# Two more groups of weight sums made ahead, and a new order of units in four feed-forward blocks

## The chip, the cores and the metric

The kernel runs on one core of one Trainium2 chip. Its time is the device time in microseconds of one execution, and the metric is the median of several. The engines of the core are named as in the profile: PE is TensorE's matmul, PEld its weight load, DVE is VectorE, ACT is ScalarE, POOL is GpSimd, and SP is SyncE, which issues most transfers. The core has 16 DMA engines.

## The reference

One decoder layer on 256 tokens of width 2048, in float32: a first half feed-forward (f1), a pair of gated token mixers (retention and sliding-window attention), a second half feed-forward (f2), and a gated per-layer embedding, each closed by a layer norm.

```python
def swiglu(x, w_gu, w_down):
    g, u = jnp.split(x @ w_gu, 2, axis=-1)
    return (jax.nn.silu(g) * u) @ w_down

for i in range(DEPTH):                                   # DEPTH = 1
    h = layer_norm(alpha * h + 0.5 * swiglu(h, w_ffn1_gu[i], w_ffn1_down[i]), ...)
    rq, rk, rv, rg, aq, ak, av, gate_r, gate_a = jnp.split(h @ w_in[i], SPLIT_POINTS, axis=-1)
    ...                                                  # retention, attention
    mixed = (sigmoid(gate_r) * ret_branch + sigmoid(gate_a) * att_branch) @ w_mix_out[i]
    h = layer_norm(alpha * h + mixed, ...)
    h = layer_norm(alpha * h + 0.5 * swiglu(h, w_ffn2_gu[i], w_ffn2_down[i]), ...)
    h = layer_norm(alpha * h + sigmoid(h @ w_ple_gate[i]) * (p[i] @ w_ple_proj[i]), ...)
```

The change concerns the weights of the two feed-forwards: `w_gu` is 2048 x 11264 (gate and up), `w_down` 5632 x 2048.

## The kernel before, in words

**A product of float32.** Every factor is split into a high and a low part, and a product is three matmuls into one sum: low of the tokens times high of the weight (line 426), high times high (L427), high times low (L428). A matmul is 128x128 by 128x512.

**Chunks.** Weights come as raw chunks of 128x1024 float32, 512 KB each, by a transfer that SP issues (L121). ScalarE casts the raw chunk to its high part (L132), VectorE subtracts to get the low part (L136).

**Blocks and units.** A feed-forward has 11 blocks of gate and up (`f1g`, `f1u`, `f2g`, `f2u`; j = 0 to 10), each with eight pairs p of chunks, one of the gate and one of the up side, and then the down product in two blocks of 22 pairs. How a pair is worked off is a letter in a string, in the order of use:

- P, a plain pair: two chunks, cast and subtracted as above, 24 matmuls.
- T, the same, but the low part of the second chunk is made without VectorE: ScalarE copies the raw chunk with its sign turned (L141), and the subtraction is a transfer with accumulation that GpSimd issues (L142). It is begun up to three units ahead.
- S, a seven: the four quarters of the pair are combined to seven products in place of eight (as Strassen does), 21 matmuls. The sums of weights are made on VectorE (four of 128x512, L216 to L218 and L221), cast on ScalarE (`huf`, L219, and `hvf`, L222; and `bf`, L207) and subtracted on VectorE (`luf` and `lvf`, L224, L225, beside L136 and L223).
- D, a prepared seven: the same 21 matmuls, but the four parts `hu`, `lu`, `hv`, `lv` were made earlier and lie in DRAM. It loads one whole chunk (L121), half of the other (L244) and four sums of 512 KB (L248); VectorE makes two low parts only.

**Sums made ahead.** `AHEAD` lists the pairs of f2's blocks that are D. `sums_ahead` makes their four parts while the token mixers run, between f1 and f2, a step at a time: each call of `run_side`, once a unit, takes one step, and `every` is the number of units between two steps. There are five stretches of the mixers in which it is started, each with a slice of the list.

**What sets the order.** The program is written out by Python in one pass. `plan` is the list of units to come; `fill` loads, then makes them ahead of their use, as long as the slots of 128x1024 that the stretch has (`slots_for_weights`) hold them and the queued matmuls stay below `ahead` = 45 and `far` = 90 in units of `time` (12 a chunk, 21 a seven). Each engine runs its own instructions in the order written, and a load waits on SP until its slot is free. So the strings decide in which order every engine meets the work, and which load stands behind which.

**After a block** VectorE and ScalarE fold the sevens' sums (`eve`, `evw`, L535 to L541), apply the gate, and turn the result by a DMA transpose that SP issues (L982).

Of the kernel before, what the change touches and what calls it, by code (L numbers as in the profile page):

```python
# [40 lines left out]

SEVEN = (0, 1, 2, 3)

AHEAD = {1: (4, 5), 2: (4,), 3: (4, 5), 4: (4,), 5: (4, 5), 7: (4, 5)}
AHEAD_SLOTS = 32

LATE = {"f1": 9, "f2": 6}

SEVEN_DOWN = (6, 7, 8, 9)
DOWN = {  # L50
    "f1": ("TTPTTPPSTSTSPSTSPSPSPP", "PTSTSTSPSPSPSPSPSPPPPP"),
    "f2": ("TTPTTPSTSTSPSTSPSPSPSP", "PTSTSTSPSPSPSPSPSPPPPP"),
}
FORMS_AT = (2, 6, 10, 14)
# [10 lines left out]
def layer(ctx: ExitStack, tc: tile.TileContext, io):  # L65
# [16 lines left out]
    def slot(shape, dt, name):  # L82
        return slots.tile(shape, dt, tag="slot", name=name)
# [179 lines left out]
    def sums_ahead(items, wait, every):  # L263


        def pause():
            for _ in range(every):
                yield

        pairs = [[Chunk(k) for k in items[0]]]  # L270
        for _ in range(wait):
            yield
        for j, (key, _) in enumerate(items):
            a, b = pairs.pop()
            b11, b21, b12, b22 = a.of(a.raw, 0), a.of(a.raw, 1), b.of(b.raw, 0), b.of(b.raw, 1)
            u, v = (slot([P, 2, 512], F32, w + a.name) for w in "uv")
            t1, t3, t2, t4 = (x.rearrange("p (g n) -> p g n", g=2) for x in (u[:, 0], u[:, 1], v[:, 0], v[:, 1]))
            parts = [slot([P, 2, 512], F32R, w + a.name) for w in ("hu", "lu", "hv", "lv")]
            uh, ul, vh, vl = parts
            away = [dram.tile([P, 2, 512], F32, name=f"{w}{a.name}") for w in ("hud", "lud", "hvd", "lvd")]  # L280
            put_by_sums[key] = away
            dve.tensor_tensor(t1, b11, b12, ALU.add)
            dve.tensor_tensor(t3, b12, b22, ALU.add)
            yield from pause()
            act.copy(uh, u)
            dve.tensor_tensor(t2, b11, t3, ALU.add)
            dve.tensor_tensor(t4, t2, b21, ALU.add)
            yield from pause()
            act.copy(vh, v)
            if j + 1 < len(items):  # L290
                pairs.append([Chunk(k) for k in items[j + 1]])
            dve.tensor_tensor(ul, u, uh, ALU.subtract)
            yield from pause()
            dve.tensor_tensor(vl, v, vh, ALU.subtract)
            for e in range(2):
                sync.dma_start(away[e], parts[e].bitcast(F32))
            yield from pause()
            for e in range(2, 4):
                sync.dma_start(away[e], parts[e].bitcast(F32))
# [52 lines left out]
    def slots_for_weights(n, ahead=45, far=90):  # L352
        room.update(slots=n, ahead=ahead, far=far)
# [5 lines left out]
    lazy = []  # L359
# [158 lines left out]
    def forms_of(parts, name):  # L518
        hi, lo = (slot([P, 8, P], F32R, name + w) for w in "hl")
        return seven_forms(whole(parts, name + "w"), hi, lo)  # L520

    def units_of(order, sevens, ahead=()):

        sevens, ahead = list(sevens), list(ahead)
        plain = [p for p in range(KD // 2) if p not in sevens + ahead]
        of = {"S": sevens, "D": ahead, "P": plain, "T": plain}
        return [(kind, of[kind].pop(0)) for kind in order]
# [399 lines left out]
    def gu_units(name, j):  # L927
        if j == 0:
            return [("P", p) for p in range(KD // 2)]
        if name == "f2" and j in AHEAD:  # L930
            if j > 4:
                return units_of("PSDSSDSP", SEVEN, AHEAD[j])
            return units_of(*(("PPSDSDSP", SEVEN[:3]) if j % 2 else ("PPSSDSSP", SEVEN)), AHEAD[j])
        return units_of("PTSSTSST" if j >= LATE[name] else "PTSSPSST", SEVEN)

    def gu_keys(name, j):
        return lambda n, p: (name + "_gu", j, n, p)
# [17 lines left out]
    def plan_ffn(name):  # L955
        for j in range(KF // 4):
            block_units(gu_units(name, j), gu_keys(name, j))
        first, second, held = down_units(name)
        block_units(first, down_keys(name, 0))
        block_units(second, down_keys(name, 1))  # L960
        plan.extend(Single(down_keys(name, 1)(n, p)) for n in range(2) for p in held)
# [30 lines left out]
    def ffn(name, i, ht, norm, keep, residual, keepers, away):  # L992
# [31 lines left out]
        for j in range(KF // 4):  # L1024
            extra = seven_banks(f"{name}{j}") if j and j % 2 == 0 else None
            pg, pu = banks(f"{name}g{j}"), banks(f"{name}u{j}")
            units = gu_units(name, j)
            n_of = {(0, 0): KD, (0, 1): KD, (1, 0): KD, (1, 1): KD}
            for kind, p in units:
# [15 lines left out]
            def before(u, j=j, offset=KD // 2 - len(units)):  # L1045
# [7 lines left out]
                if j == 0 and u == 7:  # L1053
# [3 lines left out]
                    if name == "f2":  # L1057
                        g = AHEAD[1][0] // 2
                        made[g] = forms_of([ht[:, 4 * g : 4 * g + 4, :]], f"{name}f{g}")
                if name == "f2" and j in AHEAD and u == 0:  # L1060
                    slots_for_weights(AHEAD_SLOTS - j)
# [151 lines left out]
    def mixers(ht, norm, residual, keepers, away):  # L1213
# [23 lines left out]
        def values(blk, ps):  # L1237
            hi, lo = (slot([P, 2, 512], F32R, f"rv{w}{blk}") for w in "hl")
            if isinstance(ps, list):
                for t in range(2):  # L1240
                    split(hi[:, t], lo[:, t], ps[t])
            else:
                split(hi, lo, ps)
            rv[blk] = hi, lo
# [16 lines left out]
        for n in range(2):  # L1261
            values(3 * n, ps[n])
        ahead = [(gu_keys("f2", j)(0, p), gu_keys("f2", j)(1, p)) for j in AHEAD for p in AHEAD[j]]
        slots_for_weights(22)
# [2 lines left out]
        made.clear()  # L1267
        slots_for_weights(14)
        lazy.append(rotary_table("a"))
        lazy.append(sums_ahead(ahead[0:2], 2, 2))  # L1270
        for j in range(4):
            bank(f"pass{j}")
        rq[:] = [slot([P, 4, S], F32, f"rq{j}") for j in range(2)]
# [108 lines left out]
        def two_heads(h, at=0):  # L1382
            steps = (
                ret1(h), both(ret1b(h), ret1(h + 1)), both(ret1b(h + 1), ret2(h)),
                both(ret2b(h), ret2(h + 1)), ret2b(h + 1),
            )
            for j, step in enumerate(steps):
                along(at + j, step)

        two_heads(0)  # L1390
        lazy.append(sums_ahead(ahead[2:5], 2, 3))
        for h in range(0, HR, 2):
            ps = banks(f"rg{h}")
            paired_out(("w_in_f2", grp), KD, rhs, ps)
# [132 lines left out]
            attention_features(grp)  # L1527

        slots_for_weights(14)
        lazy.append(sums_ahead(ahead[5:7], 0, 2))  # L1530
        sig = []
        for j in range(4):
            if j == 3:
# [46 lines left out]
            split(mt[:, :, :S], mt[:, :, S:], x)  # L1580

        slots_for_weights(14)
        lazy.append(sums_ahead(ahead[7:8], 0, 2))
        for j in range(4):
            v = sig[4 + j]
            act.activation(v, v, AF.Sigmoid)
# [7 lines left out]
        for b in range(2):  # L1594
# [3 lines left out]
            for n in range(2):  # L1598
                j = 2 * b + n
# [13 lines left out]

        lhs = lambda k: of_pairs(mix_t, k)
        slots_for_weights(16)
        lazy.append(sums_ahead(ahead[8:], 3, 2))
        for blk in range(3):
            if blk == 2:
                load_for_norm(1)
# [328 lines left out]
```

## Time and profile before

| what | value |
|---|---|
| median of 3 runs | 2231.51 us (2230.23 to 2231.71) |
| profiled execution | 2232.14 us, span 2230.3 us |
| granted clock of TensorE | 0.999 |
| PE busy | 2221.0 us, 10150 instructions |
| DVE busy | 1993.9 us, 89% of the span |
| ACT busy | 1434.9 us, 64% |
| transfers by hardware queue q1, most issued by SP | 530.68 MB, 71.5% of 16 engines |
| transfers with accumulation by GpSimd (q0) | 28.32 MB, 6.8%, 54 issues |
| block 9 of f2 | 1817.50 to 1858.30 us |
| first down block of f1 | its last seven near 559 us |

The profile is of one execution. An instruction's row gives its start, its duration, the engine, the line, and result and factors by the program's names, without buffer numbers. A bracket at the end of a row is idle time before it and what ended it. A row of a window gives its length, the busy time of PE, PEld, DVE, ACT and POOL with their counts, the granted clock, the share of the 16 DMA engines that is busy, and GB/s. In the trace matmuls overlap: the duration of one is longer than the distance between two.

### The profile page before, as it was taken

How to read it: one execution, taken by the hardware profiler on the slowest of the kernel's cores; microseconds unless marked ns; L12 is line 12 of the kernel's file. 1: busy time of each engine (PE TensorE's matmuls, PEld its weight loads, DVE VectorE, ACT ScalarE, POOL GpSimd, SP SyncE). 2: the span in 40 equal slices, each digit the busy share in tenths (PEclk: the TensorE clock that was granted, in tenths of full speed). 3: DMA queues.
4: the chain of work that ended last, by engine and by line, in shares of the span. 5: the costliest groups of instructions: out<-in, count | busy, mean ns of one | idle time of the engine just before them, and what ended most of it. 6: DMA issues, size and time to landing. Idle time of an engine off the chain costs nothing.

```text
span 2230.3 us, 28863 instructions
## 1 busy us (share of the span) xinstructions
PE 2221.0 (100%) x10150; PEld 1838.2 (82%) x10150; DVE 1993.9 (89%) x2649; ACT 1434.9 (64%) x1691; POOL 49.2 (2%) x63
## 2 busy tenths in 40 slices
PE   9999999999999999999999999999999999999998
PEld 8888888888888888888788888888888888888887
DVE  7999999989898998898979888699999999899878
ACT  6776777786655644566866556466658677866553
POOL 0000000000000000000000000000000000000000
PEclk9999999999999999999999999999999999999999
DMA  9788787997777668986957669798989989967771
GB/s 314 228 257 250 224 259 233 250 269 232 246 286 243 228 212 294 275 270 204 274 165 243 238 202 334 271 302 259 314 258 275 315 243 259 266 226 250 286 283 67
DMA packets 295929, 563.41 MB, mean 253 GB/s; under 512 B 94300, under 2 KB 98780, under 8 KB 295784
## 3 DMA queue, kind: packets, MB, share of 16 engines
q1 hardware_dynamic: 286024, 530.68, 71.5%
q0 software_dynamic: 7776, 28.32, 6.8%
q10 hardware_dynamic: 1984, 2.58, 0.4%
q8 instruction: 79, 1.29, 0.2%
q14 instruction: 66, 0.54, 0.1%
HBM read 484.43 MB, written 29.36 MB: 230 GB/s over the span
## 4 chain that ended last, share of the span: by engine, by line
PE 92%; DVE 4%; ACT 2%; issue 1%; DMA 1%; SPq 0%; ACTq 0%; DVEq 0%
PE f1g L428 3%; PE f1g L426 3%; PE f1g L427 3%; PE rqk L377 3%; PE f2g L426 2%; PE f2g L427 2%; PE f2g L428 2%; PE f1u L428 2%; PE f1u L426 2%; PE f1u L427 2%; PE f2u L427 2%; PE f2u L426 2%; PE f2u L428 2%; PE aqk L377 2%; PE gt L426 1%; PE f2d L428 1%
## 5 line engine op out<-in xcount | busy, mean ns | idle before, releaser
L132 ACT CAST hf_gu<-rf_gu 128x1024 fp32r<-128x1024 f32 x262 | 268.9, 1046 | 28.8 <-DMA rf_gu<-in_f_gu 28.1
L136 DVE TENSOR_TENSOR lf_gu<-rf_gu,hf_gu 128x1024 fp32r<-128x1024 f32 x228 | 272.7, 1219 | 11.6 <-ACT hf_gu L132 10.8
L132 ACT CAST hf_down<-rf_down 128x1024 fp32r<-128x1024 f32 x145 | 148.3, 1047 | 54.5 <-DMA rf_down<-in_f_down 45.2
L136 DVE TENSOR_TENSOR lw_in_f<-rw_in_f,hw_in_f 128x1024 fp32r<-128x1024 f32 x140 | 166.9, 1218 | 3.5 <-ACT hw_in_f L132 3.3
L136 DVE TENSOR_TENSOR lf_down<-rf_down,hf_down 128x1024 fp32r<-128x1024 f32 x125 | 149.9, 1220 | 7.7 <-ACT hf_down L132 6.7
L132 ACT CAST hw_in_f<-rw_in_f 128x1024 fp32r<-128x1024 f32 x140 | 142.0, 1050 | 18.0 <-DMA rw_in_f<-in_w_in_f 15.0
L222 ACT CAST hvf_gu<-vf_gu 128x1024 fp32r<-128x1024 f32 x78 | 82.3, 1055 | 82.6 <-DVE vf_gu L221 70.1
L219 ACT CAST huf_gu<-uf_gu 128x1024 fp32r<-128x1024 f32 x78 | 82.0, 1051 | 54.8 <-DVE uf_gu L217 51.3
L224 DVE TENSOR_TENSOR luf_gu<-uf_gu,huf_gu 128x1024 fp32r<-128x1024 f32 x78 | 95.1, 1219 | 4.7 <-ACT huf_gu L219 4.7
L225 DVE TENSOR_TENSOR lvf_gu<-vf_gu,hvf_gu 128x1024 fp32r<-128x1024 f32 x78 | 95.1, 1219 | 0.0
L428 PE MATMUL f1g<-lf_gu,xt 128*128 128x512 f32 x232 | 90.5, 390 | 0.3 <-DVE lf_gu L136 0.3
L426 PE MATMUL f1g<-hf_gu,xt 128*128 128x512 f32 x232 | 90.4, 390 | 0.0
L427 PE MATMUL f1g<-hf_gu,xt 128*128 128x512 f32 x232 | 90.3, 389 | 0.0
L426 PE MATMUL f2g<-hf_gu,ht 128*128 128x512 f32 x208 | 81.1, 390 | 0.0
L428 PE MATMUL f2g<-lf_gu,ht 128*128 128x512 f32 x208 | 81.0, 389 | 0.0
L427 PE MATMUL f2g<-hf_gu,ht 128*128 128x512 f32 x208 | 80.9, 389 | 0.0
L426 PE MATMUL f1u<-hf_gu,xt 128*128 128x512 f32 x192 | 74.7, 389 | 0.0
L427 PE MATMUL f1u<-hf_gu,xt 128*128 128x512 f32 x192 | 74.7, 389 | 0.0
L428 PE MATMUL f1u<-lf_gu,xt 128*128 128x512 f32 x192 | 74.7, 389 | 0.0
L142 POOL DMA_DIRECT2D lf_gu<-rf_gu x34 | 29.5, 867 | 1707.4 <-DMA rf_gu<-in_f_gu 1097.0
L377 PE MATMUL rqk<-ht,hw_in_f 128*128 128x512 f32 x256 | 64.3, 392 | 0.0
L426 PE MATMUL f2u<-hf_gu,ht 128*128 128x512 f32 x160 | 62.5, 391 | 0.0
(1632 smaller groups left out, 6870.5 us busy)
## 6 DMA issues: line engine op xcount, KB each, us to landing
rf_gu<-in_f_gu SPq DMA_DIRECT2D x360, 512.0 KB
rf_down<-in_f_down SPq DMA_DIRECT2D x176, 512.0 KB
rw_in_f<-in_w_in_f SPq DMA_DIRECT2D x148, 512.0 KB
lf_gu<-rf_gu POOLq DMA_DIRECT2D x34, 512.0 KB, 7.9
rw_rv<-in_w_rv SPq DMA_DIRECT2D x32, 512.0 KB
rw_ret<-in_w_ret SPq DMA_DIRECT2D x32, 512.0 KB
rw_mix<-in_w_mix SPq DMA_DIRECT2D x32, 512.0 KB
rw_pg<-in_w_pg SPq DMA_DIRECT2D x32, 512.0 KB
```

The lines of the kernel that those rows point to most:

```text
L132: act.copy(self.hi, self.raw)
L136: dve.tensor_tensor(self.lo, self.raw, self.hi, ALU.subtract)
L142: pool.dma_start(self.lo, self.raw.bitcast(F32R), accum_op=ALU.add)
L219: act.copy(uh, u)
L222: act.copy(vh, v)
L224: dve.tensor_tensor(ul, u, uh, ALU.subtract)
L225: dve.tensor_tensor(vl, v, vh, ALU.subtract)
L377: pe.matmul(ps[f], hi[:, kk, f * P : (f + 1) * P], rhs(k), start=k == 0, stop=k == n_k - 1,)
L426: pe.matmul(o, al, bh, start=first, stop=False)
L427: pe.matmul(o, ah, bh, start=False, stop=False)
L428: pe.matmul(o, ah, bl, start=False, stop=self.left == 0)
```

## The change

- `AHEAD` gains pairs 4 and 5 of block 9: twelve groups in place of ten. The slices of the five stretches become 3, 3, 2, 2 and 2 groups in place of 2, 3, 2, 1 and 2; in the fourth stretch a step is taken every unit in place of every second.
- f2's block 9 goes from "PTSSTSST" to "TDSSDSST": the pairs 4 and 5 are prepared sevens, pairs 6 and 7 have a low part by transfer, and three such pairs become two. The first seven is the third unit in both.
- f2's blocks 5 and 7 go from "PSDSSDSP" to "PDSSDSSP".
- f1's first down block goes to eight sevens from seven, and gets the string that f2's has.

```diff
--- before.py
+++ after.py
@@ -41,14 +41,14 @@
 
 SEVEN = (0, 1, 2, 3)
 
-AHEAD = {1: (4, 5), 2: (4,), 3: (4, 5), 4: (4,), 5: (4, 5), 7: (4, 5)}
+AHEAD = {1: (4, 5), 2: (4,), 3: (4, 5), 4: (4,), 5: (4, 5), 7: (4, 5), 9: (4, 5)}
 AHEAD_SLOTS = 32
 
 LATE = {"f1": 9, "f2": 6}
 
 SEVEN_DOWN = (6, 7, 8, 9)
 DOWN = {
-    "f1": ("TTPTTPPSTSTSPSTSPSPSPP", "PTSTSTSPSPSPSPSPSPPPPP"),
+    "f1": ("TTPTTPSTSTSPSTSPSPSPSP", "PTSTSTSPSPSPSPSPSPPPPP"),
     "f2": ("TTPTTPSTSTSPSTSPSPSPSP", "PTSTSTSPSPSPSPSPSPPPPP"),
 }
 FORMS_AT = (2, 6, 10, 14)
@@ -928,8 +928,10 @@
         if j == 0:
             return [("P", p) for p in range(KD // 2)]
         if name == "f2" and j in AHEAD:
+            if j == 9:
+                return units_of("TDSSDSST", SEVEN, AHEAD[j])
             if j > 4:
-                return units_of("PSDSSDSP", SEVEN, AHEAD[j])
+                return units_of("PDSSDSSP", SEVEN, AHEAD[j])
             return units_of(*(("PPSDSDSP", SEVEN[:3]) if j % 2 else ("PPSSDSSP", SEVEN)), AHEAD[j])
         return units_of("PTSSTSST" if j >= LATE[name] else "PTSSPSST", SEVEN)
 
@@ -1267,7 +1269,7 @@
         made.clear()
         slots_for_weights(14)
         lazy.append(rotary_table("a"))
-        lazy.append(sums_ahead(ahead[0:2], 2, 2))
+        lazy.append(sums_ahead(ahead[0:3], 2, 2))
         for j in range(4):
             bank(f"pass{j}")
         rq[:] = [slot([P, 4, S], F32, f"rq{j}") for j in range(2)]
@@ -1388,7 +1390,7 @@
                 along(at + j, step)
 
         two_heads(0)
-        lazy.append(sums_ahead(ahead[2:5], 2, 3))
+        lazy.append(sums_ahead(ahead[3:6], 2, 3))
         for h in range(0, HR, 2):
             ps = banks(f"rg{h}")
             paired_out(("w_in_f2", grp), KD, rhs, ps)
@@ -1527,7 +1529,7 @@
             attention_features(grp)
 
         slots_for_weights(14)
-        lazy.append(sums_ahead(ahead[5:7], 0, 2))
+        lazy.append(sums_ahead(ahead[6:8], 0, 2))
         sig = []
         for j in range(4):
             if j == 3:
@@ -1580,7 +1582,7 @@
             split(mt[:, :, :S], mt[:, :, S:], x)
 
         slots_for_weights(14)
-        lazy.append(sums_ahead(ahead[7:8], 0, 2))
+        lazy.append(sums_ahead(ahead[8:10], 0, 1))
         for j in range(4):
             v = sig[4 + j]
             act.activation(v, v, AF.Sigmoid)
@@ -1613,7 +1615,7 @@
 
         lhs = lambda k: of_pairs(mix_t, k)
         slots_for_weights(16)
-        lazy.append(sums_ahead(ahead[8:], 3, 2))
+        lazy.append(sums_ahead(ahead[10:], 3, 2))
         for blk in range(3):
             if blk == 2:
                 load_for_norm(1)
```

TensorE has 9946 rows in place of 9955. Two places show how the order of the other engines moves. The names end in block, side (0 gate, 1 up) and pair, and a buffer number.

SP, the loads of block 9 around the transpose of block 7's result (`f27t`), before:

```order
L121 DMA rf2_gu_9_0_4_16258<-in_f2_gu 128x2x512
L121 DMA rf2_gu_9_1_4_16274<-in_f2_gu 128x2x512
L982 DMA_TRANSPOSE f27t_16276<-f27w_16145 128x16x128
L121 DMA rf2_gu_9_0_5_16303<-in_f2_gu 128x2x512
L121 DMA rf2_gu_9_1_5_16305<-in_f2_gu 128x2x512
L121 DMA rf2_gu_9_0_0_16339<-in_f2_gu 128x2x512
L121 DMA rf2_gu_9_1_0_16341<-in_f2_gu 128x2x512
```

The same place of the changed kernel:

```order
L121 DMA rf2_gu_9_0_6_16320<-in_f2_gu 128x2x512
L121 DMA rf2_gu_9_1_6_16336<-in_f2_gu 128x2x512
L984 DMA_TRANSPOSE f27t_16338<-f27w_16207 128x16x128
L121 DMA rf2_gu_9_0_4_16368<-in_f2_gu 128x2x512
L244 DMA rf2_gu_9_0_4b_16370<-in_f2_gu 128x2x256
L248 DMA huf2_gu_9_0_4_16372<-hudf2_gu_9_0_4_12484 128x1024
L248 DMA luf2_gu_9_0_4_16374<-ludf2_gu_9_0_4_12485 128x1024
L248 DMA hvf2_gu_9_0_4_16376<-hvdf2_gu_9_0_4_12486 128x1024
L248 DMA lvf2_gu_9_0_4_16378<-lvdf2_gu_9_0_4_12487 128x1024
L121 DMA rf2_gu_9_0_0_16409<-in_f2_gu 128x2x512
L121 DMA rf2_gu_9_1_0_16411<-in_f2_gu 128x2x512
```

Between the transpose and the first seven's chunks (pair 0) stand six loads in place of two.

ScalarE, the end of block 9, with the third and the fourth seven (pairs 2 and 3) and the last pair (7), before:

```order
L219 CAST huf2_gu_9_0_2_16567<-uf2_gu_9_0_2_16565 128x1024
L222 CAST hvf2_gu_9_0_2_16569<-vf2_gu_9_0_2_16566 128x1024
L132 CAST hf2_gu_9_0_7_16596<-rf2_gu_9_0_7_16538 128x1024
L141 ACTIVATE lf2_gu_9_1_7_16598<-rf2_gu_9_1_7_16582 128x1024
L219 CAST huf2_gu_9_0_3_16603<-uf2_gu_9_0_3_16601 128x1024
L222 CAST hvf2_gu_9_0_3_16605<-vf2_gu_9_0_3_16602 128x1024
```

The same place of the changed kernel:

```order
L132 CAST hf2_gu_9_0_3_16648<-rf2_gu_9_0_3_16644 128x1024
L207 CAST bf2_gu_9_0_3_16650<-rf2_gu_9_1_3_16646 128x512
L219 CAST huf2_gu_9_0_3_16654<-uf2_gu_9_0_3_16652 128x1024
L222 CAST hvf2_gu_9_0_3_16656<-vf2_gu_9_0_3_16653 128x1024
L132 CAST hf2_gu_9_0_7_16692<-rf2_gu_9_0_7_16690 128x1024
L141 ACTIVATE lf2_gu_9_1_7_16723<-rf2_gu_9_1_7_16696 128x1024
L132 CAST hf2_gu_10_0_4_16726<-rf2_gu_10_0_4_16698 128x1024
```

The last pair's first cast and its sign-turning copy (L141) stood ahead of the fourth seven's casts `huf` and `hvf`, and now stand behind them.

## The prediction, made before the changed kernel had run

> **What bounds the kernel now.** I read the page first, then the waits of TensorE, then windows of 20 to 41 us cut at block borders, then single rows at the places the change touches.
>
> ```profile
> span 2230.3 us, 28863 instructions
> PE 2221.0 (100%) x10150; PEld 1838.2 (82%) x10150; DVE 1993.9 (89%) x2649; ACT 1434.9 (64%) x1691; POOL 49.2 (2%) x63
> PE 92%; DVE 4%; ACT 2%; issue 1%; DMA 1%; SPq 0%; ACTq 0%; DVEq 0%
> ...
> PE rv L426 <- DVE ht L792: 0.8, 1, 0.8
> PE f1d0s L428 <- DVE lvf_down L225: 0.2, 1, 0.2
> ```
>
> TensorE is busy for 2221.0 of 2230.3 us and holds 92% of the chain; behind the start no wait exceeds 0.8 us. A gain has to come out of the number of matmuls. A loss can come from any other engine or queue that starts to hold TensorE back, because nothing is idle behind it.
>
> **The price of a matmul** is the distance between two starts, not the printed duration.
>
> ```profile
> 1844.73 0.39 PE L428 MATMUL f2u<-bf_gu,f2fh 128*128 128x512 f32 x1
> 1844.95 0.39 PE L426 MATMUL f29s<-huf_gu,f2fl 128*128 128x512 f32 x1
> ...
> 1846.32 0.39 PE L426 MATMUL f29s<-hvf_gu,f2fl 128*128 128x512 f32 x1
> ```
>
> Seven steps lie between the first and the last of these rows: 1.59 / 7 = 0.227 us each. The change removes nine matmuls of this kind: a plain pair is 24, a seven or a prepared seven 21, so two pairs of block 9 and one of f1's first down block give three each. **Term 1: 9 x 0.227 = -2.0 us.**
>
> **f1's first down block** gets the string that f2's has already. Today its seventh seven is late:
>
> ```profile
> 558.00 0.39 PE L427 MATMUL f1d0s<-huf_down,f1forms 128*128 128x512 f32 x1
> ...
> 559.41 0.51 PE L428 MATMUL f1d0s<-lvf_down,f1forms 128*128 128x512 f32 x1 [0.17 <-DVE lvf_down L225]
> 559.75 0.40 PE L426 MATMUL f1d0s<-huf_down,f1forms 128*128 128x512 f32 x1
> ...
> L428 PE MATMUL f2d0s<-lvf_down,f2forms x8: 389/389/389, 1935.4 to 2004.7; 128*128 128x512 f32 x8
> ```
>
> Five steps took 1.75 us where 5 x 0.227 = 1.13 was due: 0.6 us lost. In f2, eight sevens in the new order show 389 ns for every one of the matmuls that wait longest for VectorE. **Term 2: -0.6 us** (0 if f1's VectorE is late all the same).
>
> **The sums made ahead** go from ten groups to twelve, one of them more in the first stretch of the mixers and one in the fourth, the `ma` blocks from 1225 us, where the pause between its steps falls from two to one. A group's own VectorE work is four sums of 128x512 and two differences of 128x1024; their prices come from the spacing of starts:
>
> ```profile
> 1825.48 1.22 DVE L225 TENSOR_TENSOR lvf_gu<-vf_gu,hvf_gu 128x1024 fp32r<-128x1024 f32 x1
> 1826.62 1.22 DVE L1072 TENSOR_TENSOR evw<-eve,evw 128x1024 f32<-128x1024 f32 x1
> 1827.75 0.69 DVE L216 TENSOR_TENSOR uf_gu<-rf_gu 128x512 f32<-128x512 f32 x1
> 1828.35 0.69 DVE L217 TENSOR_TENSOR uf_gu<-rf_gu,rf_gu 128x512 f32<-128x512 f32 x1
> ...
> 963.09 0.56 DVE L108 TENSOR_TENSOR rsp<-rsc,rsp 128x384 fp32r<-128x384 f32 x1
> 964.39 0.40 PE L1316 MATMUL ro<-rvh,rsp 128*128 128x256 f32 x2
> ...
> 1240.00:1300.00 60.00, 60.00 (x267) 49.67 (x266) 45.88 (x53) 33.11 (x36) 0.00 (x0) 1.00 0.68 232
> ```
>
> 1.135 us for the wide, 0.60 for the narrow: 4 x 0.60 + 2 x 1.135 = 4.7 us a group. The second new group has 14 us of VectorE to itself in the last row, a window (VectorE busy 45.88 of 60). For the first the thinnest cover I found is the score tile `rsp`, done at 963.65 and read at 964.39, 0.74 us ahead. If one operation of 1.135 slips ahead of it, 0.4 us show. **Term 3: +0.4 us** (0 to 4.7, a whole group).
>
> **Block 9, VectorE.** Up to the fourth seven VectorE has as much to do as before: a plain pair (2 x 1.135) and two pairs with a transfer (1.135 each) made 4.5 us, now one such pair and two prepared sevens (1.135 + 0.60 each) make 4.6. TensorE gets there earlier by six matmuls, 1.36 us, and the lead is this:
>
> ```profile
> 1847.01 1.22 DVE L225 TENSOR_TENSOR lvf_gu<-vf_gu,hvf_gu 128x1024 fp32r<-128x1024 f32 x1
> 1849.49 0.39 PE L428 MATMUL f29s<-lvf_gu,f2fh 128*128 128x512 f32 x1
> ```
>
> 1849.49 - 1848.23 = 1.26 us, so 0.1 to 0.2 are short. f1's rows above show what goes with a wait of that size: 0.17 is printed and 0.6 was lost over the two low parts. **Term 4: +0.6 us** (0, to 1.4 if the whole lead is lost).
>
> **Block 9, loads.** This is the main term. A prepared seven loads 512 + 256 + 4 x 512 = 2816 KB in place of two chunks of 512:
>
> ```profile
> q1 hardware_dynamic: 286024, 530.68, 71.5%
> q0 software_dynamic: 7776, 28.32, 6.8%
> ...
> huf_gu<-hudf_gu SPq DMA_DIRECT2D x10, 512.0 KB
> rf_gu_4b<-in_f_gu SPq DMA_DIRECT2D x6, 256.0 KB
> ...
> 440.00:460.00 20.00, 20.00 (x90) 16.57 (x89) 17.14 (x21) 14.23 (x16) 2.61 (x3) 1.00 1.08 286
> 1574.70:1614.80 40.10, 40.10 (x178) 33.22 (x177) 36.49 (x45) 27.74 (x31) 0.00 (x0) 1.00 0.93 310
> 1654.90:1694.50 39.60, 39.60 (x175) 32.58 (x174) 37.15 (x45) 27.11 (x30) 0.86 (x1) 1.00 0.95 297
> 1817.50:1858.30 40.80, 40.80 (x181) 33.78 (x180) 36.28 (x46) 30.22 (x33) 2.58 (x3) 1.00 0.88 252
> 1858.30:1899.30 41.00, 41.00 (x181) 33.71 (x180) 39.98 (x49) 32.67 (x36) 3.46 (x4) 1.00 0.90 247
> 1899.30:1920.00 20.70, 20.70 (x93) 17.13 (x92) 16.44 (x20) 18.76 (x20) 1.73 (x2) 1.00 1.06 315
> ```
>
> The columns of a window end with the granted clock, the DMA share and GB/s. The fourth is block 9: 0.88 x 40.8 = 35.9 us of engine time. Two prepared sevens add 2 x 1792 KB = 3.67 MB at 0.715 x 2230.3 / 530.68 = 3.005 us/MB: +11.0. One of 54 transfers falls away: 0.068 x 2230.3 / 54 = -2.8. The new block asks for 44.1 us, and TensorE's 174 matmuls last 39.5: a share of 1.12. Blocks 3 and 5, with two prepared sevens each but one transfer at most, stand at 0.93 and 0.95 and cost TensorE nothing; no stretch of a block's length exceeds that, and the highest 20 us show 1.08. So 44.1 / 0.95 = 46.4 means 7.0 us late, 44.1 / 1.08 = 40.8 means 1.4 late. I take the middle, about a share of 1.0. **Term 5: +4.2 us** (0 to 7.0). Its neighbours, 0.90 behind it and 1.06 after that, leave little to pay it back.
>
> The Trainium skill (DMA: Bandwidth & Descriptors, Specifications) gives about 358 GB/s as a core's limit at the memory. By that the block's 13.4 MB would take an estimated 37.5 us, less than TensorE's time, and this term would be zero, which is the first rival below; block 3 shows 310, and no row here reaches 358.
>
> **Block 9, the last transfer.** The second low part of its last pair comes by a negating copy on ScalarE (L141), then an adding transfer issued by GpSimd (L142). Today that copy stands ahead of the fourth seven's two casts:
>
> ```profile
> 1841.06 1.05 ACT L141 ACTIVATE lf_gu<-rf_gu 128x1024 fp32r<-128x1024 f32 x1
> 1843.11 1.05 ACT L219 CAST huf_gu<-uf_gu 128x1024 fp32r<-128x1024 f32 x1 [0.99 <-PE f2u L428]
> 1845.45 1.05 ACT L222 CAST hvf_gu<-vf_gu 128x1024 fp32r<-128x1024 f32 x1 [1.29 <-DVE vf_gu L221]
> ...
> 1842.47 0.86 POOL L142 DMA_DIRECT2D lf_gu<-rf_gu  x1 [11.94 <-DVE uf_gu L216]
> 1855.61 0.39 PE L428 MATMUL f2u<-lf_gu,ht 128*128 128x512 f32 x1
> DMA to landing us min/median/max: 6.8/7.9/9.3
> ```
>
> It is issued at 1842.47 and read at 1855.61, so 13.1 us cover a landing of 6.8 to 9.3. By the new order the copy follows `hvf` and one `hf`: from the end of `hvf`, 0.95 + 1.05 + 0.4 to the issue, then 6.8 to 9.3, so the part lands 9.2 to 11.7 us behind it. TensorE has 7.9 us until it asks: the last low part of the seven 1.2, five additions of three matmuls 3.4, the pair's first half 2.7, and half a period's steps 0.6. Late by 1.3 to 3.8. **Term 6: +2.4 us** (0 if VectorE's lead at the fourth seven is over 2 us, then `hvf` is early too). The matmuls behind it wait with it, and block 10's begin too.
>
> **Blocks 5 and 7** change the places of a seven and a prepared seven within the first three units: the same loads, sums and matmuls. Block 5 shows 39.60 of 39.60 us busy: 0, at most 0.3 either way, where a first seven falls later and its low parts gain cover.
>
> **Sum.** -2.0 - 0.6 + 0.4 + 0.6 + 4.2 + 2.4 = +5.0 us. The profiled execution, 2232.14 us (span 2230.3 and 1.8 around it), would become 2237.1; it lies 0.6 above the median, 2231.51, so on the median's scale 2236.5. A difference below 0.2%, 4.5 us, can hardly be told from none.
>
> **Rivals.**
>
> The loads fit. If what is loaded ahead holds more than some 5 us of TensorE's work, a share of 1.12 for one block is absorbed, as 1.06 and 1.08 are over 20 us without a wait. Terms 5 and 6 go (the chunk and the copy are then early), term 4 stays: -2.0 - 0.6 + 0.4 + 0.6 = -1.6, so 2229.9: not slower. It decides where the stretch of overload is shorter than the lead. For it: no row of TensorE waits on a load. Against it: on ScalarE the casts of raw chunks do wait for loads:
>
> ```profile
> L132 ACT CAST hf_gu<-rf_gu 128x1024 fp32r<-128x1024 f32 x262 | 268.9, 1046 | 28.8 <-DMA rf_gu<-in_f_gu 28.1
> ```
>
> 28.1 us over the kernel, so chunks are often cast as they land. Chance 0.30.
>
> The lateness spreads. Block 10's VectorE is busy 39.98 of 41.0 us and has four transfers: what comes late from block 9 is not made up there. With term 5 at 7.0, term 6 at 3.8 and the rest as above: +9.2, so 2240.7. It decides if the share cannot exceed 0.95 over a block. Chance 0.19.
>
> More is gained: the 0.2 us waits of f2's blocks and the new order of 5 and 7 would have to give several us; they are not in the rows. 2227, chance 0.04.
>
> That matmuls would not fall away is no case: 9946 rows stand on TensorE against 9955.
>
> **How the numbers follow.** My forecast, 2236.5, has 0.47; its own range goes from 2234 (term 5 at 1.4) to 2239. Slower by over 0.2% means 2236.0 or more: 0.33 of the forecast's 0.47, and the spread case 0.19 together 0.52. The rest of the forecast, 0.14, and the case of fitting loads, 0.30, lie within 0.2%: 0.44. Faster: 0.04. For 8 in 10 the range goes from 2229.5, so that most of the fitting loads are in, to 2241.
>
> **What would show it.** Right: in block 9's rows TensorE waits on `luf`, `lvf` or `lf` of the second and later units, VectorE or ScalarE there wait on the loads of sums or raw chunks, the window of block 9 lasts 44 us or more in place of 39.5 with a share near 1.0, and the last pair's L428 waits on GpSimd's `lf_gu`. In f1d0s, eight rows of `lvf_down` at 389. Wrong: a window of 39.5 to 40 us with a share above 1.08 (term 5), a last transfer issued before the fourth seven's first matmul (term 6), a wait above 1 us in the mixers at `ro` (term 3), or a new wait in f1's down block (term 2).

## The result

The changed kernel takes 2236.5 us (median of 16 executions, 2233.91 to 2241.51); the kernel before took 2230.82 in 16 beside it (2230.23 to 2231.94). The ratio is 1.0027, 95% interval 1.002 to 1.0034: slower, by 5.7 us. The profiled execution took 2236.4 us, span 2234.6. The forecast was 2236.5. That the number was met says little by itself, so what follows asks of each term whether it was met too. One execution of a later version, at a granted clock of 0.556 over its whole length, is left out of that version's figures.

The head of the page of the changed kernel:

```profile
span 2234.6 us, 28909 instructions
PE 2220.6 (99%) x10141; PEld 1836.4 (82%) x10141; DVE 2007.8 (90%) x2668; ACT 1440.0 (64%) x1696; POOL 48.4 (2%) x62
...
q1 hardware_dynamic: 289416, 540.65, 72.2%
q0 software_dynamic: 7632, 27.79, 6.7%
...
PE 93%; DVE 2%; DMA 2%; ACT 1%; issue 1%; ACTq 0%; DVEq 0%; SPq 0%; POOLq 0%
```

Nine matmuls are gone, 10150 to 10141, one transfer is gone, and the hardware queue moves 10 MB more. The chain now holds 2% of DMA. The waits of TensorE (line waited, releaser: total, times, longest):

```profile
PE f2u L428 <- DMA lf_gu<-rf_gu: 1.5, 1, 1.5
PE f29s L428 <- DVE lf_gu L136: 1.5, 2, 1.1
PE f29s L428 <- DVE luf_gu L224: 1.4, 1, 1.4
...
PE rv L426 <- DVE ht L792: 0.8, 1, 0.8
PE f25s L428 <- DVE luf_gu L224: 0.6, 1, 0.6
...
PE ro L1318 <- DVE rsp L108: 0.3, 1, 0.3
```

Block 9 (`f29s`, and `f2u` with the last transfer) now stands at the head of a list that had no row of block 9 before. Where the time went by place, from the first matmul of each stage in the two traces:

| stretch | TensorE, after less before | change within it |
|---|---|---|
| start of f1's first down block | +0.2 us | |
| end of it | -1.1 | -1.3 |
| value projection of attention (`av`) | -0.6 | +0.5 at `ro` |
| block 8's first seven (`f28s`) | -0.2 | +0.4, f2's blocks 5 to 8 |
| block 10's first seven (`f210s`) | +5.4 | +5.6, nearly all in block 9 |
| last matmuls | +4.5 | -0.9, small waits of before that are not met now |

Two of these points as rows, before and after (first row of each pair is f28s, the second f210s; the two times are the first and the last start). Before:

```profile
L426 PE MATMUL f28s<-huf_gu,f2fl x8: 389/389/398, 1788.8 to 1808.9; 128*128 128x512 f32 x8
L426 PE MATMUL f210s<-huf_gu,f2fl x8: 389/389/393, 1870.8 to 1890.7; 128*128 128x512 f32 x8
```

After:

```profile
L426 PE MATMUL f28s<-huf_gu,f2fl x8: 389/389/393, 1788.6 to 1808.5; 128*128 128x512 f32 x8
L426 PE MATMUL f210s<-huf_gu,f2fl x8: 389/389/389, 1876.2 to 1895.9; 128*128 128x512 f32 x8
```

82.0 us became 87.6 between the first starts, although six matmuls, 1.4 us, fell away there: block 9 loses 7.0 us. Its window in the changed kernel, from its first matmul to that of block 10:

```profile
1816.70:1863.30 46.60, 41.85 (x176) 32.06 (x175) 41.82 (x53) 30.61 (x34) 1.72 (x2) 1.00 0.99 306
```

**How block 9 loses it.** ScalarE and VectorE, ahead of the first seven of block 9 in the changed kernel (the bracket is idle time and what ended it):

```profile
1812.82 1.04 ACT L132 CAST hf_gu<-rf_gu 128x1024 fp32r<-128x1024 f32 x1
1813.77 0.58 ACT L537 COPY eve<-f28s 128x512 f32<-128x512 f32 x1
1821.54 1.05 ACT L132 CAST hf_gu<-rf_gu 128x1024 fp32r<-128x1024 f32 x1 [7.20 <-DMA rf_gu<-in_f_gu]
```

```profile
1814.38 0.69 DVE L538 TENSOR_TENSOR evw<-eve,f28s 128x512 f32<-128x512 f32 x1 [3.99 <-ACT eve L537]
...
1818.23 0.69 DVE L260 TENSOR_TENSOR bf_gu<-rf_gu_4b,bf_gu 128x512 fp32r<-128x512 f32 x1
...
1824.01 0.69 DVE L216 TENSOR_TENSOR uf_gu<-rf_gu 128x512 f32<-128x512 f32 x1 [2.71 <-DMA rf_gu<-in_f_gu]
...
1851.63 1.22 DVE L225 TENSOR_TENSOR lvf_gu<-vf_gu,hvf_gu 128x1024 fp32r<-128x1024 f32 x1
```

The first seven's raw chunks stand behind the six loads of the prepared seven, and come late: VectorE idles 2.71 us, and then works without a pause until the fourth seven's `lv`, which is ready at 1852.85. Before it was ready at 1848.23. Of the 4.6 us between, 2.7 are the wait for the chunk, 0.2 stand behind a late cast, 0.4 come from a later fold (ScalarE has one more cast ahead of its copy `eve`, that of the prepared seven's half chunk, L256), and 1.2 are work behind the fold: two prepared sevens have a second low part (`bf`, L260) of 0.6 each. TensorE would have been there 1.6 us earlier than before (1.4 for six matmuls, 0.2 that it was ahead). 4.6 + 1.6, less the lead of 1.26 that there was, is 5.0: the steps of `f29s` beyond 0.227 us sum to 5.1 us lost, of which 3.1 are printed as waits. The last two of these and the one on the transfer:

```profile
1851.76 0.50 PE L428 MATMUL f29s<-luf_gu,f2fh 128*128 128x512 f32 x1 [1.38 <-DVE luf_gu L224]
...
1852.90 0.50 PE L428 MATMUL f29s<-lvf_gu,f2fh 128*128 128x512 f32 x1 [0.17 <-DVE lvf_gu L225]
...
1860.84 0.50 PE L428 MATMUL f2u<-lf_gu,ht 128*128 128x512 f32 x1 [1.54 <-DMA lf_gu<-rf_gu]
```

That transfer was issued at 1853.31 by GpSimd, behind the fourth seven's casts, where before it was issued at 1842.47.

What the DMA engines did meanwhile (windows of the changed kernel; the last three columns are clock, DMA share and GB/s):

```profile
1790.00:1800.00 10.00, 10.00 (x46) 8.29 (x45) 7.83 (x10) 10.00 (x12) 0.00 (x0) 1.00 0.59 185
...
1811.50:1824.00 12.50, 12.50 (x57) 10.36 (x56) 6.79 (x10) 3.90 (x5) 0.00 (x0) 1.00 1.04 362
1824.00:1832.00 8.00, 7.91 (x35) 6.25 (x34) 7.88 (x11) 7.52 (x8) 0.00 (x0) 1.00 0.99 348
```

They had room at 0.59 twenty microseconds earlier and are full when the chunks are wanted. The trace shows a crowd at one place; that the block would be too heavy on average it does not show.

### The profile page after: what moved, and what is told of

The parts are those of the page before. It is cut to its first block, busy times and chain, and to the rows that moved or that the text cites. A ratio compares the mean times of both kernels' runs of the same rounds, so it can differ in the third digit from the quotient of the medians.

```text
span 2234.6 us, 28909 instructions
## 1 busy us (share of the span) xinstructions
PE 2220.6 (99%) x10141; PEld 1836.4 (82%) x10141; DVE 2007.8 (90%) x2668; ACT 1440.0 (64%) x1696; POOL 48.4 (2%) x62
## 4 chain that ended last, share of the span: by engine, by line
PE 93%; DVE 2%; DMA 2%; ACT 1%; issue 1%; ACTq 0%; DVEq 0%; SPq 0%; POOLq 0%
PE f1g L428 3%; PE f1g L426 3%; PE f1g L427 3%; PE rqk L377 3%; PE f1u L428 2%; PE f1u L426 2%; PE f1u L427 2%; PE f2g L426 2%; PE f2g L427 2%; PE f2g L428 2%; PE f2u L428 2%; PE f2u L426 2%; PE f2u L427 2%; PE aqk L377 2%; DMA rf_gu<-in_f_gu 1%; PE gt L426 1%
## 5 line engine op out<-in xcount | busy, mean ns | idle before, releaser
L426 PE MATMUL f2g<-hf_gu,ht 128*128 128x512 f32 x202 | 78.7, 390 | 0.0
L427 PE MATMUL f2g<-hf_gu,ht 128*128 128x512 f32 x202 | 78.6, 389 | 0.0
L428 PE MATMUL f2u<-lf_gu,ht 128*128 128x512 f32 x152 | 59.3, 390 | 1.5 <-DMA lf_gu<-rf_gu 1.5
```

What stands on the lines that cost most here:

```text
L426: pe.matmul(o, al, bh, start=first, stop=False)
L427: pe.matmul(o, ah, bh, start=False, stop=False)
L428: pe.matmul(o, ah, bl, start=False, stop=self.left == 0)
```

## The experiments

All were timed beside the kernel before (2230.9 to 2231.2 us in these comparisons). For block 9 these theories stood against each other: loads that come late at one place, too little bandwidth over the block, and VectorE with too little time whatever the loads do. The last transfer, f1's string, and the order of blocks 5 and 7 were taken apart from them.

### f1's string alone

```diff
-    "f1": ("TTPTTPPSTSTSPSTSPSPSPP", ...
+    "f1": ("TTPTTPSTSTSPSTSPSPSPSP", ...
```

> The kernel before with f1's first down block in the new string and nothing else. My account of the changed kernel's trace: f1's down block starts 0.18 us later than before and ends 1.14 earlier, so it gives 1.3 us (three matmuls 0.68, the wait at 559 us 0.6). Expected: 1.3 us faster than before, eight rows of lvf_down in f1d0s at 389 ns. If the gain of the changed kernel there hung on something else of the change, 0 to 0.7.

Measured: 2229.25 us (2228.94 to 2230.26, 11 executions) against 2231.18, ratio 0.9992, interval 0.9983 to 1.0. In its trace f1's down block gives 1.3 us; the further 0.6 to 1.7 that it is ahead later are small waits of before (blocks 6 to 8 and the end) that it does not meet. No wait at `ro` is in its trace. The eight sevens of f1 in the changed kernel, against 0.51 us for the last of seven before:

```profile
L428 PE MATMUL f1d0s<-lvf_down,f1forms x8: 389/389/389, 494.5 to 563.8; 128*128 128x512 f32 x8
```

### Blocks 5 and 7 alone

```diff
-                return units_of("PSDSSDSP", SEVEN, AHEAD[j])
+                return units_of("PDSSDSSP", SEVEN, AHEAD[j])
```

> The kernel before with blocks 5 and 7 in the order PDSSDSSP and nothing else. The prediction had 0, at most 0.3. In the changed kernel's trace the last seven of block 5 waits 0.8 us on luf and lvf (1.2 us lost), and block 6 loses 0.8 less than before. If that wait comes from the order: +0.3 to +0.5 us net, and a wait on luf_gu in f25s of about 0.6. If it came from the sums of block 9 being made or from the chip's jitter: 0 and no such wait.

Measured: 2231.03 us against 2231.18, ratio 0.9999 (0.9991 to 1.0008): no change to be told from noise. The wait of 0.6 on `luf` in block 5 is not in its trace, so the order alone does not make it. In the changed kernel it comes, 1.2 us are lost there, and 0.8 of them are given back in block 6.

### The two groups and block 9 alone

f1's string and the order of blocks 5 and 7 as before, the rest as changed.

> The changed kernel with f1's string and the order of blocks 5 and 7 as before: only the two groups more and block 9's string. By addition: changed 2236.5, plus 1.3 for f1, minus 0.4 for blocks 5 and 7, so 2237.4, 6.6 us above before. Block 9 loses 6.9 us of waits and wins 1.4 from six matmuls; the wait at ro gives 0.5.

Measured: 2236.53 us (2235.55 to 2243.43), ratio 1.0025 (1.0016 to 1.0034). The whole loss is in this part, 5.4 us against 6.6 expected. The parts do not add: -1.9, -0.2 and +5.4 make +3.3, where the whole showed +5.7. The interval of each part is about 2 us to either side, so a difference of 2.4 is not told from noise. The profiled execution was the slowest of the eleven, 2243.43, and shows what makes such an execution slow, in two windows, in TensorE's waits and in the steps of its matmuls:

```profile
1853.60:1857.00 3.40, 3.39 (x8) 2.65 (x9) 2.73 (x3) 3.40 (x5) 0.86 (x1) 0.53 1.19 261
...
1865.50:1868.90 3.40, 3.34 (x8) 2.67 (x9) 0.00 (x0) 0.00 (x0) 0.00 (x0) 0.50 1.03 283
```

```profile
PE f2u L428 <- DMA lf_gu<-rf_gu: 3.9, 1, 3.9
```

```profile
1854.47 0.63 PE L427 MATMUL f29s<-huf_gu,f2fh 128*128 128x512 f32 x1
1854.90 0.63 PE L428 MATMUL f29s<-luf_gu,f2fh 128*128 128x512 f32 x1
```

Behind the waits the granted clock is 0.53 and 0.50, and matmuls start some 0.43 us apart in place of 0.227. The last transfer was waited for 3.9 us instead of 1.5.

### Half of the prepared sums not loaded

```diff
+                if few and w[0] == "l":          # few: block 9
+                    self.sums.append(self.sums[-1])
+                    continue
                 t = slot([P, 2, 512], F32R, w + self.a.name)
                 sync.dma_start(t.bitcast(F32), v)
```

> The changed kernel, but the two prepared sevens of block 9 load only hu and hv of their sums and use them in place of lu and lv as well: 2 MB less to load, the same matmuls and VectorE work (the weight sums' low parts are left out). Loads theory: the six loads ahead of the first seven's chunks make VectorE idle 2.7 us, and this is what it cannot make up; without it the fourth seven's low part is ready at 1850.0 in place of 1852.85, where TensorE without a wait would ask at 1847.9. So 2 us of waits are left there and 1.5 at the last transfer: 2.9 us faster than the changed kernel, 2233.6. Bandwidth alone (the prediction's term 5, all of the waits but the transfer's): 5.2 us faster, 2231.3. VectorE theory (its own work sets the waits, whatever the loads do): within 0.7 us of the changed kernel.

Measured: 2233.87 us (2231.77 to 2241.89), ratio 1.0014 (1.0006 to 1.0023): 2.6 us less than the changed kernel, as the loads theory had it and neither of the others. In its trace the steps of `f29s` lose 2.2 us in place of 5.1. VectorE's idle time ahead of the first seven is gone; the seven starts as soon as the gate is done:

```profile
1818.44 1.28 DVE L1076 TENSOR_TENSOR evw<-evw,f2u 128x512 f32<-128x512 f32 x2
1819.63 0.69 DVE L216 TENSOR_TENSOR uf_gu<-rf_gu 128x512 f32<-128x512 f32 x1
```

But waits of TensorE are left, so loads are not all of it:

```profile
PE f2u L432 <- DMA lf_gu<-rf_gu: 2.6, 1, 2.6
PE f29s L432 <- DVE luf_gu L224: 1.4, 1, 1.4
```

Each prepared seven has two loads fewer and so holds two slots fewer as well; no run separates the two.

### Less work on VectorE

```diff
+            if a.key[:2] == ("f2_gu", 9) and a.key[-1] in (0, 1, 2):
+                vl = vh
+            else:
                 dve.tensor_tensor(vl, v, vh, ALU.subtract)
```

> The changed kernel, but the first three sevens of block 9 use hv in place of lv, so VectorE makes no lv for them (the low part of two weight sums is left out): 3 x 1.135 = 3.4 us less VectorE work before the fourth seven, the same loads and matmuls. If the waits inside block 9 are VectorE running with no slack from the late first seven on: 5.1 us of waits shrink by 3.4, so 2233.1 (the last transfer's wait stays). If the matmuls wait on the arrival of the prepared sums themselves: no change, 2236.5. If loads are late again and again through the block, VectorE would idle in place of working and less than 1 us is won.

Measured: five executions from 2233.47 to 2244.15, median 2238.07, ratio 1.0039 (1.0025 to 1.0053). The median contradicts all three expectations. The profiled execution is the fastest and fits the first to 0.4 us: 2.2 us lost in `f29s` in place of 5.1, and a wait of 1.7 on the transfer. This did not settle it by itself; a later run does.

### The last pair plain

`"TDSSDSST"` became `"TDSSDSSP"`.

> The changed kernel with block 9 as TDSSDSSP: the last pair's low part is made on VectorE (1.135 us more there) in place of by transfer. If term 6 is what the trace shows, the wait on lf_gu's transfer (1.5 us printed, 1.7 lost, more in other executions) goes and nothing comes in its place: 2234.6. If the transfer's time on the DMA engines also held up the loads, a little more. If VectorE has no room there: a wait on lf_gu of the last pair, and 2236 or more.

Measured: 2235.17 us (2233.45 to 2238.28), ratio 1.0021 (1.0012 to 1.0029): 1.3 us less than the changed kernel, 0.6 short of the expectation. That is little beside the spread of both; what carries the reading is the trace, where no wait on `lf_gu`'s transfer is left and none came in its place at the last pair.

### Transposes on ScalarE's queue

```diff
-        sync.dma_start_transpose(turns, parts.rearrange("p w n -> p (w n)"))
+        act.dma_start_transpose(turns, parts.rearrange("p w n -> p (w n)"))
```

> The changed kernel with the DMA transposes issued on ScalarE's queue in place of SP's: the loads behind a transpose no longer wait with it (4.8 us at block 9's first prepared seven). If the loads are late because they are issued late: VectorE's 2.7 us of idle time ahead of the first seven go, 2.9 us faster, 2233.6. If they are late because the 16 engines are full (356 GB/s in the 20 us ahead): they start earlier and end no earlier, within 0.7 of 2236.5. If the issue costs ScalarE time where it has none: slower by up to 2.

Measured: 2327.66 us, ratio 1.0437. None of the expectations. TensorE waits 19.7 us for two transfers of `lf_gu` alone, and their landing times reach 24.1 us where the changed kernel's longest was 10.0:

```profile
PE f2u L428 <- DMA lf_gu<-rf_gu: 19.7, 2, 16.8
PE f1d L428 <- DMA lf_down<-rf_down: 7.5, 1, 7.5
```

```profile
DMA to landing us min/median/max: 4.8/8.1/24.1
```

Moving the transposes changed far more than the loads' start. Why the transfers land so late was not tried, and whether the loads of block 9 would be early enough if only issued earlier stays open.

### One prepared seven, none ahead of the first seven

f1's string; block 9 as `"TTSSDSST"` with pair 4 prepared; blocks 5 and 7 in the old order; eleven groups, the eleventh in the fourth stretch.

> A version meant to keep the gains: f1's string; blocks 5 and 7 in the old order; block 9 as TTSSDSST with one prepared seven, behind the second seven, so that no prepared loads stand ahead of the first seven's chunks; eleven groups, the eleventh in the fourth stretch, so that the first has no more work than before. Six matmuls fewer than before. If loads ahead of the first seven and VectorE's lost cover are the cause, block 9 has no wait over 0.3 us and the time is f1_only's 2229.25 less 0.7: 2228.6. If any second prepared load overloads the block (share 35.9 + 5.5 = 41.4 of 40.1 us): waits of 1 to 3 us on lf or lvf in f29s, 2230 to 2232.

Measured: 2237.12 to 2239.44 us in four executions, ratio 1.0035 (1.0021 to 1.0049). The gains were not kept. VectorE never idles for a load inside block 9, and waits come all the same:

```profile
PE f2u L428 <- DMA lf_gu<-rf_gu: 3.7, 1, 3.7
...
PE f29s L428 <- DVE luf_gu L224: 1.3, 1, 1.3
PE f29s L428 <- DVE lf_gu L136: 0.4, 1, 0.4
```

```profile
1815.27 0.69 DVE L538 TENSOR_TENSOR evw<-eve,f28s 128x512 f32<-128x512 f32 x1 [6.59 <-ACT eve L537]
```

VectorE has less work than before, but it idles 6.59 us ahead of block 8's fold, where before it idled 2.05. That idle time ends with ScalarE's copy `eve`, and ScalarE stood behind a load. The row of ScalarE ahead of that copy with f1's string alone, in this version, and in the next one:

```profile
1809.66 1.06 ACT L141 ACTIVATE lf_gu<-rf_gu 128x1024 fp32r<-128x1024 f32 x1 [2.04 <-PE f2g L427]
```

```profile
1811.81 1.06 ACT L141 ACTIVATE lf_gu<-rf_gu 128x1024 fp32r<-128x1024 f32 x1 [4.29 <-DMA rf_gu<-in_f_gu]
```

```profile
1812.07 1.06 ACT L141 ACTIVATE lf_gu<-rf_gu 128x1024 fp32r<-128x1024 f32 x1 [4.42 <-DMA rf_gu<-in_f_gu]
```

In these three TensorE begins block 8's sevens within 0.2 us of each other, and the fold begins at 1812.17, 1815.27 and 1814.59. So a load is late here too, a raw chunk that ScalarE waits for, and VectorE gets the delay through the fold: 3.1 us of it, and 0.6 for the second low part of the one prepared seven, make the 3.7 us by which the fourth seven's `lvf` is later than with f1's string alone (1850.13 against 1846.44). Prepared loads ahead of the first seven are not needed for it. Why this chunk lands late was not found out.

### The first unit plain

`"TTSSDSST"` became `"PTSSDSST"`.

> one_prepared with its first unit plain in place of a transfer (PTSSDSST for TTSSDSST): VectorE gets 1.135 us more work, at a place where it is idle (one_prepared: 6.6 us ahead of the fold of block 8). If lost cover at the front is what starves VectorE, the idle time falls by about 2, the waits in f29s too, and the kernel is 1.5 to 2.5 us faster than one_prepared (2239.4, its fastest 2237.1): 2236 to 2237.5. If VectorE's amount of work counts: slower than one_prepared by about 1.

Measured: 2236.88 us (2232.08 to 2237.39), ratio 1.0023 (1.0015 to 1.0032), 2.1 to 2.5 below the version above, as the first expectation had it. Its trace carries that only in part: the idle time ahead of the fold is 4.64 in place of 6.59, and the printed waits in `f29s` fall from 1.9 to 1.5, but the last transfer is now waited for 4.1 us, and the two profiled executions differ by 0.2 us only. The first unit is now the one of the kernel before, and the fold is still 2.4 us later than with f1's string alone, by the load in the rows above. So the lost low part is not the main thing that made the first version slow; and 1.135 us more of VectorE's work, at a place where it idles, cost nothing.

### Less work on VectorE and the last pair plain

> b9_less_dve (no lv for the first three sevens of block 9, the low part of two sums left out) with the last pair plain in place of a transfer. b9_less_dve showed waits of 0.8 us in block 9 in its profile, 5.1 in the changed kernel's, and 1.7 at the last transfer, but its times went from 2233.5 to 2244. If the transfer's wait and the slow clock that follows a long wait make that spread: 2231.5, all executions within 2 us. If VectorE's work is not the cause and the profile was a lucky execution: 2235 (b9_last_plain's) with its spread.

Measured: 2231.59 us (2230.83 to 2233.36, 11 executions), ratio 1.0003 (0.9994 to 1.0012). 3.6 us less than with the last pair plain alone, for 3.4 us of VectorE work. The traces give somewhat less: the steps of `f29s` lose 2.1 us here and 4.6 there (outside a stretch of slow clock), and 2.2 against 5.1 in the pair with the transfer. So VectorE has next to no slack in block 9, and 2.5 to 2.9 of the 3.4 us show. All of this work was there before the change too, so it says how little room there is, not how much of the loss VectorE's new work made. The spread of 10 us is gone with the transfer's wait.

### All three taken away

> The changed kernel with all three suspected causes taken away in block 9: half of the prepared sums not loaded, no lv for the first three sevens, the last pair plain (the low parts of several weight sums are left out). If these three are the whole loss, no wait over 0.3 us is left in block 9 and the time is the kernel before less nine matmuls and f1's wait, plus 0.5 at ro: 2231.0 - 2.0 - 0.6 + 0.5 = 2228.9, with f1_only's narrow spread. If something else costs time there: above 2230.

Measured: 2229.66 us (2228.73 to 2230.66), ratio 0.9993 (0.9985 to 1.0002); no wait in block 9 is left in the list, `ro` waits 0.2. It is 0.8 above the 2228.9 that was expected. With the three taken away the loss in block 9 is gone; the half of the loads is worth 1.9 us here, where it was 2.6 with the others in place.

### The same nine matmuls elsewhere

f1's string; block 9, blocks 5 and 7 as before; a second prepared seven in f2's block 2 and a fourth seven in block 1.

```diff
-AHEAD = {1: (4, 5), 2: (4,), ...
+AHEAD = {1: (4, 5), 2: (4, 5), ...
-            return units_of(*(("PPSDSDSP", SEVEN[:3]) if j % 2 else ("PPSSDSSP", SEVEN)), AHEAD[j])
+            return units_of(*ORD[j], AHEAD[j])   # ORD[1] "PSDSSDSP", ORD[2] "PDSSDSSP", the others as before
-        lazy.append(sums_ahead(ahead[7:8], 0, 2))
+        lazy.append(sums_ahead(ahead[7:9], 0, 1))
```

> A version that takes the same nine matmuls away where VectorE and the transfers have room: f1's string, block 9 and blocks 5 and 7 as before, the eleventh group in f2's block 2 (second prepared seven, share 0.81 there, PDSSDSSP), and a fourth seven in block 1 (VectorE busy 35.5 of 40.1 us, PSDSSDSP). If the place is what counts: f1_only's 2229.25 less 6 x 0.227 = 1.4, so 2227.9, no new wait over 0.3. If block 1's or 2's VectorE (40.0 of 40.1 us in block 2) has no slack: waits in f21s or f22s, 2229 to 2232.

Measured: 2228.4 us (2227.23 to 2231.62, 11 executions) against 2230.9, ratio 0.999, interval 0.9982 to 0.9999: faster than both kernels, 2.5 us below the one before. The waits of TensorE, the three longest:

```profile
PE warm L1825 <- POOL ident masks.py:199: 1.4, 1, 1.4
PE rv L427 <- DVE ht L793: 0.9, 1, 0.9
PE pln L1717 <- DVE plnst L1715: 0.2, 1, 0.2
```

Two windows of 40 us, from 4 to 5 us ahead of the first matmul of block 1 and of block 2:

```profile
1488.00:1528.00 40.00, 40.00 (x178) 33.11 (x177) 39.86 (x49) 24.69 (x30) 0.00 (x0) 1.00 0.80 279
1528.00:1568.00 40.00, 40.00 (x178) 33.13 (x177) 38.25 (x47) 27.24 (x31) 0.00 (x0) 1.00 0.97 299
```

The second stands at a DMA share of 0.97, the first at 39.86 of 40.0 us of VectorE, and TensorE waits for neither. Nine matmuls by 0.227 are 2.0 us, of 2.5 gained.

## Why the prediction was right, and where it was not

The sum was +5.0 us on the profiled execution's scale; the traces differ by 4.5 at the last matmul, the medians by 5.7. The forecast was reckoned from a median of 2231.51, and the kernel before measured 2230.82 beside the changed one: a change 0.7 us larger than forecast met a start 0.7 lower, and that the two figures are the same is luck. The signs that were named came: block 9's window lasts 46.6 us at a share of 0.99, TensorE waits on `lf`, `luf` and `lvf` there, ScalarE and VectorE wait on raw chunks, and the last pair waits for GpSimd's transfer; none of the signs against it came.

- **Terms 1 and 2** (-2.0, -0.6): right. Nine matmuls fewer; f1's down block gave 1.3 us, the three matmuls and the 0.6.
- **Term 3** (+0.4): right, 0.5 at `ro`, and none where the first stretch makes no more than before (f1's string alone, one prepared seven, the last version).
- **Blocks 5 and 7** (0): right, -0.2 us alone by the medians, and +0.4 over blocks 5 to 8 in the changed kernel's trace.
- **Term 6** (+2.4): right in its mechanism, a copy that now stands behind `hvf`. The profiled wait cost 1.7 us, the median changed by 1.3 without it. With the same block 9 another execution waited 3.9 (block 9 alone), and the version with a plain first unit 4.1, above the 3.8 of the bound. The bound took landings of 6.8 to 9.3 us from one window; over the whole trace of before the transfers of `lf_gu` took 6.0 to 10.3.
- **Terms 4 and 5** (+0.6 and +4.2): their sum, 4.8, is near what TensorE loses in `f29s`, 5.1. Each was off. By the split above VectorE would have been 1.9 us short without the loads (1.2 of work, 0.4 of the later fold and 1.6 of TensorE's earlier arrival, less the lead of 1.26), and the loads made 2.9. The step of term 4 that failed is "Up to the fourth seven VectorE has as much to do as before". The amounts were right, 4.5 and 4.6, but not the places: the 1.1 us saved on the first unit fell into time that VectorE spends idle ahead of block 8's fold (2.05 us before, 3.99 after), and the 1.2 us added by the second low parts stand behind it. The cover in front of the first seven was counted as if it could be spent later.
- **Term 5's reasoning** from a block's mean share was also wrong in kind. It rests on "no stretch of a block's length exceeds that", meaning 0.95, and the trace of before has 40 us at 1.07 in which TensorE does not wait:

```profile
440.00:480.00 40.00, 40.00 (x178) 33.13 (x177) 33.34 (x39) 33.64 (x36) 4.33 (x5) 1.00 1.07 298
```

So the bound of 7.0 us and the condition of the spreading rival, a share that cannot exceed 0.95 over a block, had no ground; and a share of 1 is no limit, since rows here go up to 1.81. By 1.07 the same working gives 44.1 / 1.07 = 41.2, 1.7 us late. (Its own bounds, 46.4 and 40.8 less 39.5, are 6.9 and 1.3, not 7.0 and 1.4.) In the trace of the changed kernel the engines stand at 0.59 around 1795 us and at 1.04 at 1811 to 1824. The loads cost 2.6 us with the rest in place, 1.9 without, and 2.9 in the trace: late at one place, ahead of the first seven.

So two errors, term 4 too small by about 1.3 us and term 5 too large by as much, met in the total, and that is luck. What was right for its own reasons is the direction: the matmuls give 2 us, and no stage of block 9 had room for what the change moved into it.

The rival of the fitting loads fell. The Trainium skill's figure in DMA: Bandwidth & Descriptors (Specifications), about 358 GB/s at the memory, is near the rate of the crowd: its 12.5 us show 362, all transfers counted, the 8 us behind them 348. It is no ceiling of what is moved here, since a later stretch of 3.4 us shows 404, all transfers counted. But such a rate does not save the block, since the loads are asked for unevenly; the bytes of a block over that rate say only what would be possible. The rival of a lateness that spreads fell as well in the profiled execution: behind block 9 TensorE keeps its distance to the end. The slowest executions reach that rival's 2240.7 in another way: in the one that was profiled, by the clock and a longer wait on the last transfer.

## What the runs showed that had not been expected

**The clock falls behind a wait.** In five profiled versions (block 9 alone, half of the sums, the last pair plain, one prepared seven, the first unit plain) TensorE ran for 3.4 us at about half its speed after waits in block 9, and in the first of them for 6.8 us more. The half-sums version, the 3.4 us ahead of the drop and the 3.4 of it, and, for comparison, the same place of the changed kernel:

```profile
1844.80:1848.20 3.40, 1.87 (x8) 0.91 (x6) 3.40 (x5) 2.35 (x3) 0.00 (x0) 1.00 1.05 386
1848.20:1851.60 3.40, 3.40 (x9) 2.43 (x10) 3.39 (x3) 3.40 (x5) 0.86 (x1) 0.53 1.17 268
```

```profile
1849.50:1852.90 3.40, 1.86 (x7) 0.90 (x7) 3.40 (x5) 2.90 (x4) 0.00 (x0) 1.00 1.05 404
1853.60:1857.00 3.40, 3.40 (x17) 2.80 (x16) 2.72 (x3) 3.40 (x5) 0.57 (x1) 1.00 1.81 257
```

With the same 1.86 us or so of TensorE's work in 3.4 us, the clock fell once and once not. Eight steps of about 0.43 us in place of 0.227 cost 1.6 us, so one wait of 1.4 us can cost 3. The Trainium skill (TensorE: Matmul & The Clock Gate, Part 1: The HAM clock gate) tells of a window of about 3.4 us that runs free of the kernel, by which such a drop would depend on where the waits fall in it; the length agrees with the trace, where the drops last 3.41 us or twice that. It puts the half clock behind an idle window. Two of the five agree, with nearly no matmul in the 3.4 us ahead of the drop (waits of 3.7 and 4.1 us); in the other three it came behind 3.4 us that were busy for some 1.9. Such drops, with longer waits on the last transfer, are the likely reason for the spread of the changed kernel, 2233.9 to 2241.5: its three executions above 2240 have a mean clock of 0.998, the others mostly 0.999. One drop of 1.6 us would not make the 5 us by itself. The drops were seen in traces of its variants only; of the changed kernel's own slow executions there is no trace.

**A transfer's landing varies more than one window of before showed:** 6.8 to 9.3 us at block 9 before, 10.3 one block ahead of it, and 10.2 to 11.5 at block 9 in the slowest profiled execution. Why was not found out.

## What to carry to other kernels

Where an engine has no slack, count its work by place: what is saved in time that it idles anyway saves nothing, and what is added behind that time is paid in full. A mean share of the DMA engines over a block does not tell whether its loads are late; look at the ten microseconds ahead of the first use, and at what stands ahead of it in the queue. A load that is late need not show as a wait of the engine that loses by it: follow an idle time back to what ended it, and that in turn. With nine matmuls fewer the kernel became 2.5 us faster where six of them were taken from blocks with room, and 5.7 slower where they were taken from one without; and a wait of a microsecond can be charged twice, the second time by the clock.
